# A decoder layer on one core: input projection in three parts, twenty up pairs half ahead, and modulation columns placed by running estimates

## The chip, the cores and the metric

One core of a Trainium2 chip runs the whole layer in one launch. The metric is device time in microseconds, the median of several runs. A profile of one execution stands beside it. TensorE does the matmuls (PE in the rows, PEld for its weight loads), VectorE is DVE, ScalarE is ACT, and SyncE (SP) issues all DMAs of this kernel in one queue.

## What is computed

One layer on 256 tokens of width 2048, all in float32. A conditioning vector c gives six modulation vectors; the layer has eight stick-breaking heads, eight sparse heads with an indexer, an output projection and a gated FFN of width 5504 with a causal convolution of width 3.

```python
mod = silu(c) @ w_ada + b_ada                    # (2048) x (2048, 6 * 2048)
sh1, sc1, g1, sh2, sc2, g2 = split(mod, 6)
h = rmsnorm(x, norm1_g) * (1 + sc1) + sh1
proj = h @ w_in                                  # q, k, v of 8 heads; q, k, v of the sparse heads; indexer
o_sb = stick_breaking_attention(q_sb, k_sb, v_sb)
o_ds = dsa_attention(rope(q_ds), rope(k_ds), v_ds, rope(q_ix), rope(k_ix), w_ix)   # top 64 keys
x = x + g1 * (concat(rmsnorm(o_sb), rmsnorm(o_ds)) @ w_out)
h2 = rmsnorm(x, norm2_g) * (1 + sc2) + sh2
x = x + g2 * ((silu(gate) * val) @ w_down)       # gate, val = split(conv3(h2 @ w_up))
return rmsnorm(x, final_norm_g)
```

## The kernel before

**Numbers in two halves.** Every large matmul is made in fp32r from a high and a low half of each operand. split() (L143) takes a weight tile that load() (L135) has brought into one of four raw buffers: ScalarE casts the high half (L149), VectorE subtracts it for the low half (L150). nat() (L153) and trn() (L175) then issue three matmuls (high by high, high by low, low by high). fold() (L161) does the same with two: one of 512 columns for both halves of the activations and one of 256.

**The modulation vectors.** They are 96 columns of 128 numbers; column j needs 1 MiB of w_ada. ada(j) (L227) loads it and makes the column on VectorE by one multiply with a running sum (L229). ada_pe (L198) makes four columns on TensorE in four steps of 1 MiB; PEG (L44) names those groups, five of them. Columns 0 to 31 are needed by the input projection (k and 16 + k for k-tile k), 32 to 47 by the residual after the output projection, 48 to 79 by the FFN's input (48 + k and 64 + k), and 80 to 95 after the FFN.

**Who places them.** The columns stand in two lists, `pending` and `pend_pe`. pump() (L382) is called between loads; its n-th call emits as many of each list as the n-th digit of two strings in PLAN (L48) says. need(j) (L395) emits until column j is out.

**The input projection** runs in two parts of eight k-tiles (PARTS, L46). do_A (L412) walks the k-tiles of a part and makes h for each (h_make, L339), with eight PSUM banks; do_A2, do_V and do_QK follow with the same k-tiles. put() (L350) copies the sums of the first part to SBUF on ScalarE and adds those of the second part on VectorE.

**Attention.** After A2 of the last part the sparse attention is traced (L522 to L664), then V and QK of the last part with the stick-breaking heads (sb_head, L670). PSUM is split into four banks for sums and four for attention.

**Output projection and FFN.** do_O (L714) runs in two half steps, with the first half of four output tiles ahead of the norm of the stick-breaking heads. resid() (L738) adds the residual and gathers squares; rms_b (L109) and h2_make (L772) then make h2. do_U (L804) makes one pair of up tiles in two halves of eight k-tiles. The first halves of pairs 0 to 7 (G0 = 8, L801) are made first, each holding one PSUM bank, so that only k-tiles 0 to 7 of h2 are needed; then the second halves follow. Pairs 0 to 7 use trn, the others fold. The down projection streams 43 tiles.

**Order.** The program is traced in the order of the code, and a scheduler then puts each engine's instructions in a fixed queue: among those that its own model holds ready it takes the one traced first. On the chip every queue runs in that order.

Of the kernel before, what the change touches and what calls it, by code (L numbers as in the profile page):

```python
# [19 lines left out]
P = 128  # L20
D = 2048
S = 256
# [32 lines left out]
def layer(ctx: ExitStack, tc: tile.TileContext, a, out):  # L55
# [12 lines left out]
    def sm(n, name):  # L68
        return wp.tile([P, n], F32, name=name, tag="sm", bufs=8)

# [37 lines left out]

    def rms_b(sqs_, width, y, name, tag):  # L109
# [25 lines left out]
    def load(src, n, name):  # L135
# [25 lines left out]
    def fold(steps):  # L161

        lo_first = narrow[0] and not any(s[4] for s in steps)
# [32 lines left out]
    def ada_pe(j0, q, st={}):  # L198
# [4 lines left out]
        w = load(a["wg"][PEG.index(j0), q], 2048, f"wg{j0}{q}")  # L203
# [23 lines left out]
    def ada(j):  # L227
        w = load(a["wa"][j], 2048, f"wa{j}")
# [69 lines left out]

    def rope(x, t, H, rd, o, name):
# [12 lines left out]
    def modulate(dh, dl, x, am, rb, sh, name, variant):  # L312

        h = s2([P, S], F32, name)
        if not variant:
# [33 lines left out]

    def put(half, dst, src, scale=1.0):  # L350
# [5 lines left out]
        elif scale == 1.0:  # L356
# [5 lines left out]
    credit = [0.0, 0.0]  # L362
# [17 lines left out]
    step = [0]  # L380

    def pump():  # L382
        i = step[0]
        step[0] += 1
        for c, l in enumerate((pending, pend_pe)):
            if i < len(PLAN[c]):
                n = int(PLAN[c][i])
            else:
                credit[c] += RATE[c]
                n = int(credit[c])  # L390
                credit[c] -= n
            for _ in range(min(n, len(l))):
                emit(l)
# [73 lines left out]
    def do_QK(pi, h):  # L467
        n = PARTS[pi]
        acc = ps(f"QK{pi}{h}", tag=ptag[0])
        if n <= 8:  # L470
            w = load(a[f"wQK_{pi}"][h], 2 * n * P, f"wQK{pi}{h}")
        for p_ in range(2):
            o = p_ * n * P
            if n > 8:
                w = load(a[f"wQK_{pi}"][h][:, o:o + n * P], n * P, f"wQK{pi}{h}{p_}")
                o = 0
            for j0 in range(0, n, 8):
                nj = min(8, n - j0)
                wh, wl = split(w, o + j0 * P, nj * P, f"wQK{pi}{h}{p_}{j0}")
                for j in range(j0, j0 + nj):  # L480
                    trn(acc[:, p_ * S:(p_ + 1) * S], hp(hh, pi, j), hp(hl, pi, j),
                        wh[:, (j - j0) * P:(j - j0 + 1) * P], wl[:, (j - j0) * P:(j - j0 + 1) * P], j == 0, j == n - 1)
# [35 lines left out]
    psum_pool[0] = (pool2, {"acc": 4, "att": 4})  # L518
    ptag[0] = "acc"


    for t in range(NT):  # L522
# [19 lines left out]
    sc_n = [0]  # L542
    pump()

# [5 lines left out]
    for t in range(NT):  # L550
# [27 lines left out]
        V.tensor_tensor(out=sacc[0], in0=sacc[0], in1=sacc[1], op=ALU.add)  # L578
        cur, nxt = sacc
# [7 lines left out]
        V.tensor_tensor(out=mb[t], in0=mb[t], in1=cmt, op=ALU.add)  # L587
        pump()

# [17 lines left out]
    for t in range(NT):  # L607
# [29 lines left out]
        for g in range(2):  # L637
# [6 lines left out]
            for j in range(4):  # L644
                h = 4 * g + j
                A.activation(od[:, h, t * P:(t + 1) * P], pv[:, j, :], AF.Copy, scale=par[:, PDG + h:PDG + h + 1])
        pump()
    for w_ in (4, 2):
# [5 lines left out]

    def norm_o(o, rb_, oh, ol):
# [316 lines left out]
```

## Time and profile before

| what | value |
|---|---|
| median of three runs | 1203.6 us (1203.34 to 1205.74) |
| the profiled execution | 1204.37 us, its span 1202.6 us |
| mean granted TensorE clock | 0.982 |
| TensorE busy | 1150.5 us (96%) |
| VectorE busy | 880.1 us (73%) |
| ScalarE busy | 635.3 us (53%) |
| HBM | 300.24 MB read, 251 GB/s over the span |

A matmul's end is modelled, so a busy TensorE is not TensorE at its peak; the rate is read from the starts. Busy times of VectorE and ScalarE overlap a little from one instruction to the next, so that a duration and the distance of two starts differ. "Idle before" names what ended an engine's wait.

### The profile page before, as it was taken

To read this page: it belongs to the slowest core of one execution; us is meant where nothing else is said; L and a number is where in the kernel's file an instruction comes from. 1 tells how busy PE (TensorE), PEld (TensorE's weight loads), DVE (VectorE), ACT (ScalarE), POOL (GpSimd) and SP (SyncE) were. 2 spreads that over 40 slices of the span, in tenths; PEclk is the share of its full clock that TensorE was granted. 3 is DMA by queue.
4 is the path that set the end of the run, shared out by engine and by line. 5 is a ranking of instruction groups with operands and counts; after the bars stand their busy time and mean duration, and the time that the engine had idled before them with its cause. 6 is when DMAs were issued, how large, how long until landed. Compare 5 with 4: busy or idle time off the path is not lost.

```text
span 1202.6 us, 17743 instructions
## 1 busy us (share of the span) xinstructions
PE 1150.5 (96%) x7120; PEld 1014.9 (84%) x7120; DVE 880.1 (73%) x1267; ACT 635.3 (53%) x1004; POOL 0.2 (0%) x4
## 2 busy tenths in 40 slices
PE   4699999899999998999999999999999999999996
PEld 2578997668879997999888888888888888888885
DVE  4886788699868888978788878787787645545453
ACT  3356554458566444556665565565556544444441
POOL 0000000000000000000000000000000000000000
PEclk9799999999999998999999999999999999999998
DMA  8988989758788796966578657565665555455531
GB/s 321 365 322 318 340 331 350 288 198 328 279 314 321 295 344 250 353 227 231 187 283 313 229 207 264 211 241 213 242 214 184 201 180 202 179 193 193 181 135 70
DMA packets 43283, 303.49 MB, mean 252 GB/s; under 512 B 4928, under 2 KB 5440, under 8 KB 7232
## 3 DMA queue, kind: packets, MB, share of 16 engines
q1 hardware_dynamic: 43200, 302.35, 68.2%
q8 instruction: 56, 0.92, 0.3%
q14 instruction: 27, 0.22, 0.0%
HBM read 300.24 MB, written 2.10 MB: 251 GB/s over the span
## 4 chain that ended last, share of the span: by engine, by line
PE 91%; DVE 4%; ACT 3%; DMA 1%; issue 1%; SPq 0%; DVEq 0%
PE U L172 21%; PE W L172 13%; PE U L170 11%; PE W L170 7%; PE U L178 3%; PE U L179 3%; PE QK L177 3%; PE U L177 3%; PE O L177 3%; PE O L179 3%; PE O L178 3%; PE QK L178 3%; PE QK L179 3%; PE A L155 2%; DVE wa L229 2%; PE A L156 2%
## 5 line engine op out<-in xcount | busy, mean ns | idle before, releaser
L229 DVE SCALAR_TENSOR_TENSOR wa<-wa,scb 128x2048 f32<-128x2048 f32 x76 | 173.4, 2284 | 2.2 <-DMA wa<-wa 2.1
L848 ACT COPY u<-U 128x256 f32<-128x256 f32 x70 | 26.1, 372 | 116.6 <-PE U L172 116.6
L849 DVE TENSOR_TENSOR u<-U,u 128x256 f32<-128x256 f32 x70 | 29.4, 420 | 58.7 <-ACT u L848 58.7
L859 DVE SCALAR_TENSOR_TENSOR uc<-u,par,uc 128x255 f32<-128x255 f32 (+1 forms) x140 | 63.8, 478 | 0.9
L855 ACT ACTIVATE uc<-u,par 128x256 f32<-128x256 f32 x70 | 41.9, 601 | 0.0
L866 ACT CAST aT<-uc 128x256 fp32r<-128x256 f32 x43 | 17.4, 404 | 33.3 <-DVE uc L865 33.3
L894 DVE SCALAR_TENSOR_TENSOR x1T<-W,mod,x1T 128x256 f32<-128x256 f32 x16 | 7.7, 482 | 31.1 <-PE W L170 31.1
L745 ACT ACTIVATE x2q<-x1T 128x256 f32<-128x256 f32 x15 | 6.3, 418 | 38.7 <-DVE x1T L740 38.6
L327 ACT ACTIVATE amul<-mod,b,par 128x1 f32<-128x1 f32 x32 | 12.0, 385 | 27.7 <-DVE wa L229 27.7
L206 PE MATMUL ap<-wg,csil 128*32 128x512 f32 x160 | 24.0, 657 | 0.7 <-DMA wg<-wg 0.4
L861 ACT ACTIVATE uc<-uc 128x256 f32<-128x256 f32 x43 | 17.9, 416 | 7.7 <-DVE uc L859 7.6
L330 ACT ACTIVATE mod<-mod,par 128x1 f32<-128x1 f32 x32 | 8.7, 295 | 24.0 <-DVE wa L229 22.9
L865 DVE TENSOR_TENSOR uc<-uc 128x256 f32<-128x256 f32 x43 | 18.2, 423 | 2.8
L867 DVE TENSOR_TENSOR aT<-uc,aT 128x256 fp32r<-128x256 f32 x43 | 18.0, 418 | 0.8 <-ACT aT L866 0.7
L859 DVE SCALAR_TENSOR_TENSOR uc<-U,par,uc 128x255 f32<-128x255 f32 (+1 forms) x32 | 15.0, 478 | 1.0 <-ACT uc L855 0.6
L206 PEld LDWEIGHTS ap<-wg,csil 128*32 128x32 f32 x160 | 4.4, 116 | 9.8 <-issue 7.4
L559 PE MATMUL rel<-ws,qixT 64*128 64x128 f32 (+1 forms) x64 | 9.7, 399 | 1.5 <-ACT rl L564 1.5
L576 DVE SCALAR_TENSOR_TENSOR scw<-rl,wix,scw 128x128 f32<-128x128 f32 (+1 forms) x28 | 10.4, 409 | 0.0
L287 PE MATMUL cb<-ident,csil 128*128 128x128 f32 x16 | 3.6, 423 | 7.1 <-DMA ident<-ident 7.1
L211 ACT COPY rw<-ap 128x512 f32<-128x512 f32 x5 | 2.9, 586 | 14.1 <-PE ap L206 14.1
L155 PE MATMUL A<-wA00h,hh 128*128 128x512 f32 x4 | 2.5, 671 | 8.1 <-ACT hh L322 8.1
L855 ACT ACTIVATE uc<-U,par 128x256 f32<-128x256 f32 x16 | 9.0, 560 | 2.3 <-DVE uc L859 2.3
(2810 smaller groups left out, 4025.3 us busy)
## 6 DMA issues: line engine op xcount, KB each, us to landing
wU<-wU SPq DMA_DIRECT2D x86, 1024.0 KB, 4.8
wa<-wa SPq DMA_DIRECT2D x76, 1024.0 KB, 5.8
wD<-wD SPq DMA_DIRECT2D x43, 1024.0 KB, 4.6
wg<-wg SPq DMA_DIRECT2D x20, 1024.0 KB, 7.2
wA<-wA SPq DMA_DIRECT2D x16, 1024.0 KB, 7.4
wQK<-wQK SPq DMA_DIRECT2D x16, 1024.0 KB, 6.6
wO<-wO SPq DMA_DIRECT2D x16, 1024.0 KB, 6.9
xT<-xT SPq DMA_DIRECT2D x4, 512.0 KB, 5.8
```

Source lines behind the costliest of these rows:

```text
L155: T.matmul(pt, lhsT=xh, rhs=wh, start=first, stop=False)
L170: T.matmul(pt[:, 1, :], lhsT=wl, rhs=x[:, 0, :], start=False, stop=stop)
L172: T.matmul(pt, lhsT=wh, rhs=x, start=first, stop=stop)
L177: T.matmul(pt, lhsT=wh, rhs=xh, start=first, stop=False)
L178: T.matmul(pt, lhsT=wh, rhs=xl, start=False, stop=False)
L179: T.matmul(pt, lhsT=wl, rhs=xh, start=False, stop=last)
L206: T.matmul(pt[32 * j:32 * j + 32, :], lhsT=csil[:, k:k + 1].to_broadcast([P, 32]), rhs=w[:, j * 512:(j + 1) * 512], start=q == 0, stop=q == 3)
L229: i = V.scalar_tensor_tensor(out=w, in0=w, scalar=1.0, in1=scb, op0=ALU.mult, op1=ALU.mult, accum_out=mod[:, j:j + 1])
L848: A.copy(out=u[:, gv, :], in_=acc[gv][:, 1, :])
L849: V.tensor_tensor(out=u[:, gv, :], in0=acc[gv][:, 0, :], in1=u[:, gv, :], op=ALU.add)
L855: A.activation(uc[:, gv, :], u[:, gv, :], AF.Identity, scale=par[:, PCW + 3 * i + 2:PCW + 3 * i + 3], bias=par[:, PCB + i:PCB + i + 1])
L859: V.scalar_tensor_tensor(out=uc[:, gv, sft:S], in0=u[:, gv, 0:S - sft], scalar=par[:, o:o + 1], in1=uc[:, gv, sft:S], op0=ALU.mult, op1=AL ...
```

## The change

The input projection runs in three parts of 4, 6 and 6 k-tiles. The first halves of 20 up pairs, not 8, are made ahead; each is copied from PSUM to a tile `ut` in SBUF at once, and the second half is added to it. PEG keeps two groups, 40 and 44, and they may be emitted only once the input projection's A stages are over (`open_pe`). PLAN is gone: pump() now keeps three running estimates, of TensorE's, VectorE's and the DMA's time (`clk`), which every traced step advances (`spend`), and emits a column when the DMA and VectorE are estimated far enough ahead of TensorE. V of the last part is traced ahead of the sparse attention. The sparse attention, the heads, put, resid, rope, the norms and the modulation of h2 are marked: traced within tc.high_priority(), so that the scheduler takes them ahead of unmarked instructions that are ready. PSUM is split five to three in the middle stage, and five output tiles have their first half ahead.

```diff
-PEG = [4, 40, 48, 76, 52]
-PARTS = [8, 8]
-PLAN = ("40300000010011011020201102100000000000000010222000110020002020001010003012011002101000000000100000213",
-        "00000000000000000000000000000110010000001200000100001200003100000000000000110100001010001000001000000")
-RATE = (0.4, 0.7)
+PEG = [40, 44]
+PARTS = [4, 6, 6]
+G0 = 20
...
+    def ahead(f):
+        def g(*args, **kw):
+            with tc.high_priority():
+                return f(*args, **kw)
+        return g
...
+    clk = {"pe": 0.0, "dve": 0.0, "dma": 8.0}
+    def spend(pe=0.0, dve=0.0):
+        clk["pe"] += pe
+        clk["dve"] = max(clk["dve"], clk["pe"] - 10.0) + dve
+    def load(src, n, name, weight=True):
+        if weight:
+            pump()
+        clk["dma"] = max(clk["dma"], clk["pe"] - 14.0) + 3.04 * n / 2048
+        if weight:
+            clk["pe"] = max(clk["pe"], clk["dma"] + 5.0)
+            spend(0.0, 2.45 * n / 2048)
         w = wp.tile([P, 2048], F32, name=name, tag="raw", bufs=4)
...
     def nat(pt, xh, xl, wh, wl, first, last):
+        spend(3 * (pt.shape[-1] + 32) / 2400)
...
     def trn(pt, xh, xl, wh, wl, first, last):
+        spend(0.36)
...
     def ada(j):
-        w = load(a["wa"][j], 2048, f"wa{j}")
+        w = load(a["wa"][j], 2048, f"wa{j}", False)
+        spend(0.0, 2.4)
...
     def pump():
-        i = step[0]
-        step[0] += 1
-        for c, l in enumerate((pending, pend_pe)):
-            if i < len(PLAN[c]):
-                n = int(PLAN[c][i])
...
+        for _ in range(2):
+            if clk["dma"] + 11.5 > clk["pe"]:
+                return
+            if pending and clk["dve"] + 6.0 <= clk["pe"]:
+                emit(pending)
             else:
+                if pend_pe and open_pe[0]:
+                    emit(pend_pe)
+                return
...
-        natural(pi, a[f"wV_{pi}"][g], 512, 4, acc, f"V{pi}{g}")
+        natural(pi, a[f"wV_{pi}"][g], 512, 4 if PARTS[pi] % 4 == 0 else 3, acc, f"V{pi}{g}")
...
-    psum_pool[0] = (pool2, {"acc": 4, "att": 4})
+    psum_pool[0] = (pool2, {"acc": 5, "att": 3})
     ptag[0] = "acc"
+    open_pe[0] = True
+    for g in range(2):
+        do_V(last_p, g)
+    begin()
     for t in range(NT):
         rope(a2[:, t, 0:ID].rearrange("p (h d) -> p h d", h=1)[:, :, 0:16], t, 1, 16, 32, f"ki{t}")
...
-    for g in range(2):
-        do_V(last_p, g)
     for h in range(NH):
         do_QK(last_p, h)
...
-    acc = [ps(f"O{m}", tag="acc") for m in range(4)]
-    for m in range(4):
+    acc = [ps(f"O{m}", tag="acc") for m in range(5)]
+    for m in range(5):
...
-    G0 = 8
-    uacc = {}
+    uacc, ut = {}, []
     def do_U(f, i):
-        if i == 0:
-            uacc[f] = [bank(f"U{f}{gv}") for gv in range(2)] if f >= G0 else bank(f"U{f}")
+        if f < G0:
+            uacc[f] = bank(f"U{f}{i}")
+        elif i == 0:
+            uacc[f] = [bank(f"U{f}{gv}") for gv in range(2)]
...
     for f in range(G0):
         do_U(f, 0)
-        pump()
+        if f % 4 == 0:
+            ut.append(b8([P, 4, 2, S], F32, f"ut{f}"))
+        A.copy(out=ut[-1][:, f % 4, :, :], in_=uacc.pop(f))
...
         else:
-            u = acc
+            u = ut[f // 4][:, f % 4, :, :]
+            V.tensor_tensor(out=u, in0=acc, in1=u, op=ALU.add)
```

begin() and end() open and close the same mark around the sparse attention; pump() is called between an end() and the next begin(). put, rms_b, rope, norm_o, sb_head, resid and the modulate of h2 are wrapped by ahead().

## Rows read from the trace of the kernel before

**Rows 1.** The page's first part: busy us, share of the span, instructions.

```profile
span 1202.6 us, 17743 instructions
...
PE 1150.5 (96%) x7120; PEld 1014.9 (84%) x7120; DVE 880.1 (73%) x1267; ACT 635.3 (53%) x1004; POOL 0.2 (0%) x4
```

**Rows 2.** Busy time by stage: length, engines' busy us, PEclk, DMA share, GB/s.

```profile
0.00:57.00 57.00, 29.54 (x111) 19.66 (x112) 36.40 (x78) 22.28 (x40) 0.20 (x4) 0.85 0.90 342
57.00:92.80 35.80, 33.94 (x145) 26.44 (x144) 27.84 (x34) 20.39 (x34) 0.00 (x0) 1.00 0.88 333
92.80:168.00 75.20, 75.20 (x529) 71.44 (x528) 57.95 (x57) 43.77 (x71) 0.00 (x0) 1.00 0.86 324
168.00:222.00 54.00, 53.75 (x262) 43.69 (x264) 40.64 (x46) 22.61 (x33) 0.00 (x0) 1.00 0.91 339
222.00:262.00 40.00, 34.73 (x208) 22.35 (x201) 34.70 (x129) 19.50 (x35) 0.00 (x0) 0.91 0.61 232
...
372.00:458.00 86.00, 86.00 (x720) 86.00 (x719) 74.55 (x89) 42.80 (x63) 0.00 (x0) 1.00 0.87 322
...
466.00:511.70 45.70, 45.37 (x363) 45.08 (x363) 44.35 (x59) 22.79 (x36) 0.00 (x0) 0.95 0.83 314
511.70:557.80 46.10, 46.10 (x386) 46.10 (x386) 36.82 (x57) 27.86 (x43) 0.00 (x0) 1.00 0.64 233
```

**Rows 3.** TensorE in order of time, 5 to 60 us: start, us, instruction.

```profile
34.27 1.22 PE L155 MATMUL A<-wA00h,hh 128*128 128x512 f32 x2 [8.10 <-ACT hh L322]
...
56.88 0.39 PE L155 MATMUL A<-wA20h,hh 128*128 128x512 f32 x1
...
57.56 0.39 PE L155 MATMUL A<-wA20h,hh 128*128 128x512 f32 x1
```

**Rows 4.** Other engines in order of time, first 30 us.

```profile
4.49 2.60 SPq L137 DMA_DIRECT2D wg<-wg  x4
...
12.99 1.55 ACT L288 COPY scb<-cb 128x512 f32<-128x512 f32 x3
...
14.69 0.68 DVE L197 TENSOR_TENSOR sq<-sq 128x512 f32<-128x512 f32 x1
...
29.71 2.29 DVE L229 SCALAR_TENSOR_TENSOR wa<-wa,scb 128x2048 f32<-128x2048 f32 x1 [0.79 <-DMA wa<-wa]
```

**Rows 5.** The chain that ended last, one up pair of 35: start, us.

```profile
564.19 3.83 PE U L170 x32
568.02 7.28 PE U L172 x32
```

**Rows 6.** TensorE in order of time, 220 to 263 us.

```profile
221.76 1.92 PE L206 MATMUL ap<-wg,csil 128*32 128x512 f32 x16
224.39 0.66 PE L214 MATMUL aq<-ident,rw 128*128 128x128 f32 x4 [0.71 <-ACT rw L211]
...
235.40 0.79 PE L155 MATMUL V<-V1000h,hh 128*128 128x512 f32 x1
```

**Rows 7.** VectorE in order of time: split, two columns, partial sums, convolution steps.

```profile
55.43 1.23 DVE L150 TENSOR_TENSOR wA21l<-wA,wA21h 128x1024 fp32r<-128x1024 f32 x1 [0.39 <-ACT wA21h L149]
56.57 2.28 DVE L229 SCALAR_TENSOR_TENSOR wa<-wa,scb 128x2048 f32<-128x2048 f32 x1
...
58.78 2.29 DVE L229 SCALAR_TENSOR_TENSOR wa<-wa,scb 128x2048 f32<-128x2048 f32 x1
...
207.93 2.48 DVE L357 TENSOR_TENSOR qix<-A,qix 128x512 f32<-128x512 f32 x4
...
554.14 0.99 DVE L859 SCALAR_TENSOR_TENSOR uc<-U,par,uc 128x255 f32<-128x255 f32 x2
...
556.92 0.42 DVE L867 TENSOR_TENSOR aT<-uc,aT 128x256 fp32r<-128x256 f32 x1
```

**Rows 8.** DMA issues: count, KB each, median us to landing.

```profile
wQK<-wQK SPq DMA_DIRECT2D x16, 1024.0 KB, 6.6
...
xT<-xT SPq DMA_DIRECT2D x4, 512.0 KB, 5.8
```

More of the change, by code (lines that the diff above doesn't have):

```diff
@@ L69, in sm, with begin, end @@
         return wp.tile([P, n], F32, name=name, tag="sm", bufs=8)
+    def ahead(f):
[3 more added lines that the diff above has]
+        return g
+    guard = []
+    def begin():
+        guard.append(tc.high_priority())
+        guard[-1].__enter__()
+    def end():
+        guard.pop().__exit__(None, None, None)
     psum_pool = [None]
@@ L107, in rb @@
         return wp.tile([P, S], F32, name=name, tag="rb", bufs=2)
+    @ahead
     def rms_b(sqs_, width, y, name, tag):
@@ L161, in fold @@
     def fold(steps):
+        spend(0.348 * len(steps))
         lo_first = narrow[0] and not any(s[4] for s in steps)
@@ L202, in ada_pe @@
         pt = st[j0]
-        w = load(a["wg"][PEG.index(j0), q], 2048, f"wg{j0}{q}")
+        w = load(a["wg"][PEG.index(j0), q], 2048, f"wg{j0}{q}", False)
+        spend(0.85 if q < 3 else 1.4)
         for j in range(4):
@@ L297, in layer @@
                            op1=ALU.mult)
+    @ahead
     def rope(x, t, H, rd, o, name):
@@ L314, in modulate @@
         h = s2([P, S], F32, name)
+        spend(0.0, 0.9)
         if not variant:
@@ L348, in layer @@
     qk = [b8([P, 8, S], F32, f"qk{i}") for i in range(2)]
+    @ahead
     def put(half, dst, src, scale=1.0):
@@ L355, in put @@
                 A.mul(out=dst, in_=src, mul=scale)
-        elif scale == 1.0:
+            return
+        spend(0.0, 0.53)
+        if scale == 1.0:
             V.tensor_tensor(out=dst, in0=src, in1=dst, op=ALU.add)
@@ L378, in emit @@
             emitted.update(range(j, j + 4))
-    step = [0]
+    open_pe = [False]
     def pump():
-        i = step[0]
-        step[0] += 1
-        for c, l in enumerate((pending, pend_pe)):
-            if i < len(PLAN[c]):
-                n = int(PLAN[c][i])
-            else:
[L389 to L393, printed above, removed]
+        for _ in range(2):
[3 more added lines that the diff above has]
+                emit(pending)
+            else:
+                if pend_pe and open_pe[0]:
+                    emit(pend_pe)
+                return
     def need(j):
@@ L469, in do_QK @@
         acc = ps(f"QK{pi}{h}", tag=ptag[0])
-        if n <= 8:
-            w = load(a[f"wQK_{pi}"][h], 2 * n * P, f"wQK{pi}{h}")
+        w = load(a[f"wQK_{pi}"][h], 2 * n * P, f"wQK{pi}{h}")
         for p_ in range(2):
-            o = p_ * n * P
-            if n > 8:
-                w = load(a[f"wQK_{pi}"][h][:, o:o + n * P], n * P, f"wQK{pi}{h}{p_}")
+            if p_ == 0 or n > 4:
+                wh, wl = split(w, p_ * n * P, min(2, 8 // n) * n * P, f"wQK{pi}{h}{p_}")
                 o = 0
[L477 to L482, printed above, removed]
+            else:
+                o = n * P
+            for j in range(n):
+                sl = slice(o + j * P, o + (j + 1) * P)
+                trn(acc[:, p_ * S:(p_ + 1) * S], hp(hh, pi, j), hp(hl, pi, j), wh[:, sl], wl[:, sl], j == 0, j == n - 1)
         dst = qk[h // 4]
@@ L542, in layer @@
     sc_n = [0]
+    end()
     pump()
+    begin()
     def sc_t(L, name):
@@ L587, in layer @@
         V.tensor_tensor(out=mb[t], in0=mb[t], in1=cmt, op=ALU.add)
+        end()
         pump()
+        begin()
     for t in range(NT):
@@ L646, in layer @@
                 A.activation(od[:, h, t * P:(t + 1) * P], pv[:, j, :], AF.Copy, scale=par[:, PDG + h:PDG + h + 1])
+        spend(10.0, 5.0)
+        end()
         pump()
+        begin()
     for w_ in (4, 2):
@@ L653, in layer @@
     odl = b8([P, NH, S], F32R, "odl")
+    @ahead
     def norm_o(o, rb_, oh, ol):
@@ L661, in norm_o @@
             V.tensor_tensor(out=ol[:, sl, :], in0=o[:, sl, :], in1=oh[:, sl, :].bitcast(F32), op=ALU.subtract)
+            spend(0.0, 2.5)
     norm_o(od, rdb, odh, odl)
+    end()
     pump()
+    begin()
+    end()
     os_ = b8([P, NH, S], F32, "os")
     sbt = b8([P, D], F32, "sbt")
+    @ahead
     def sb_head(h):
+        spend(3.0, 1.6)
         q = qk[h // 4][:, (h % 4) * 2, :]
@@ L736, in layer @@
     sq2 = ws[:, 1536:1792]
+    @ahead
     def resid(dst, acc, gate, res, sqsum, k, name):
+        spend(0.0, 0.9)
         resid_i[0] = V.scalar_tensor_tensor(out=dst, in0=acc, scalar=gate, in1=res, op0=ALU.mult, op1=ALU.add)
@@ L780, in h2_make @@
         sh = mod_cols(k, 64, 48, am, PN2, b2)
-        modulate(h2[k // 4][:, k % 4, 0, :], h2[k // 4][:, k % 4, 1, :], x1T[i][:, j, :], am, r2p if k < 3 else r2, sh,
+        ahead(modulate)(h2[k // 4][:, k % 4, 0, :], h2[k // 4][:, k % 4, 1, :], x1T[i][:, j, :], am, r2p if k < 3 else r2, sh,
                  f"g2_{k}", False)
@@ L821, in do_U @@
                 else:
-                    trn(uacc[f][:, gv, :], x[:, 0, :], x[:, 1, :], wh[:, sl], wl[:, sl], k == 0 and gv == 0,
-                        k == KT - 1 and gv == 1)
+                    trn(uacc[f][:, gv, :], x[:, 0, :], x[:, 1, :], wh[:, sl], wl[:, sl], j == 0 and gv == 0,
+                        j == 7 and gv == 1)
         fold(steps)
```

7 lines of the change are left out of this document (3 added, 4 removed).

## The prediction

> **What bounds the kernel now.** I read the page's first part, then busy time by stage, then the stretches in which TensorE is not gapless. TensorE is busy for 1150.5 of the span's 1202.6 us, VectorE for 880.1 [rows 1]. By stage [rows 2], TensorE has almost no idle time from 57 us on: 1.9 us up to 92.8, 0.3 in 168 to 222, none in the output projection (372 to 458) and none in the second up halves (511.7 to 557.8). From there to the last down matmul it streams one up pair in 7.28 + 3.83 = 11.11 us [rows 5]. So the time moves in three ways only: less TensorE work, less idle time ahead of 57 us, or less loss in the attention stretch (222 to 262). Three resources stand just behind it: the DMA engines move 324 to 342 GB/s (0.86 to 0.91 of their time) in each stage up to 222, and VectorE is busy 74.6 of 86.0 us in the output projection and 44.4 of 45.7 us in the first up halves [rows 2]. A change that hands them work can lose what TensorE gains.
>
> At the start TensorE begins the A projection at 34.27 us and only at 56.88 has it done two k-tiles [rows 3]. A k-tile is 24 matmuls of 512 columns; three take 57.56 - 56.88 = 0.68 us at the full clock, so it is 5.44 us of work, and 22.6 us went by for 10.9.
>
> **The change, part by part.** The sum is made against the profiled execution, 1204.4 us (span 1202.6 and 1.8 around it), 0.8 above the median of 1203.6.
>
> *Start.* PEG loses group 4, so four 1 MiB loads that are issued at 4.49 us leave the head of SP's queue [rows 4] and the first two modulation columns take their place. VectorE can begin them when ScalarE's last scb copy ends (12.99 + 1.55 = 14.5) and its own square sums end (14.69 + 0.68 = 15.4). Two columns at 2.21 us start to start [rows 7] end at 19.8; today the first matmul comes 34.27 - 32.00 = 2.3 us after the second column [rows 3, 4], so A starts at about 22.5 instead of 34.3. Each further k-tile needs 3 MiB (two columns, one wA): 3.15 MB at 342 GB/s [rows 2] is 9.2 us; VectorE needs 2 x 2.21 + 2 x 1.14 and two modulation steps of 0.4, some 7.5 us, so the DMA sets the pace. Part 0 now ends after four k-tiles: 22.5 + 3 x 9.2 + 5.4 = 55. At 55 four are done where two were at 56.9: **12.8 us ahead** (2 x 5.44 + 1.9). Bounds 9 and 15: A starting 3 us later, or 373 GB/s (below).
>
> *Parts of 6 and 6.* While TensorE does A2, V and QK of part 0 (37.6 us: 3.7, 10.9 and 23.0, by their columns and the matmul rates of [rows 2, 3]), the DMA must bring their weights and the columns of part 1. From k-tile 3 on to the weights of k-tile 9 that is 1.3 + 2 + 4 + 12 + 6 = 25.3 MiB, or 26.5 MB; at 324 GB/s, the lowest rate of these stages, 82 us, at 339 / 0.91 = 373, all engines busy all the time, 71 us [rows 2], where TensorE has 37.6 + 32.6 = 70 us of work. For part 2 it is 29 MiB in 82 to 94 us against 89. Stall 1 to 17; at 342 it is 7.5 and 0, I take **8 us lost**. Stepping the new planner's three clocks through the loads gives the order: 6 of part 1's 12 columns are issued ahead of its A stage, 8 of part 2's 12; the rest come within it. Extra partial sums on VectorE, 30 of them, are 14 us by the row of four in 2.48 us for the wide ones [rows 7] and an estimated 0.35 for QK's at half that width; VectorE was busy 40.6 of 54.0 us in 168 to 222 [rows 2], so they fit, and cost 0 to 4 us, in the far bound.
>
> *PE groups.* Outside the start four groups become two. A group is 32 matmuls, twice 1.92, and its transposes, 0.66 [rows 6], with 0.7 us of wait between: 4.5 to 5.2 us. **9.3 us gained.** In return twelve more columns go to VectorE and SP carries the same bytes; 12 x 2.21 = 26.5 us, whose cover is the far larger time until the second up halves: G0 = 20 gives 20 first halves, 115 us, to the last sixteen columns. Today there are eight, 46 us.
>
> *Attention.* In 222 to 262 TensorE idles 5.3 us and its granted clock is 0.91, so some 7 us at the lower level (1.2 GHz) [rows 2], and the first V matmul comes only at 235.40 [rows 6]. Now V of the last part is traced ahead of the attention, so 16 us of matmuls stand there without waiting. The loss of about 8.7 us can come back between 0 and 6; **3 gained**. The marks move instructions within their queues and add none; what a marked instruction waits for, everything behind it on ScalarE or VectorE waits for too, split() above all, and TensorE behind that.
>
> *Up pairs.* Twelve more pairs use trn, three matmuls of 256 columns, in place of fold. trn takes 86.00 / 720 = 0.119 us per matmul [rows 2], 0.358 per step; fold 11.11 / 32 = 0.347 [rows 5]. 12 x 32 x 0.011 to 0.013 = **4.6 us lost** (4.2 to 5). The Trainium skill (TensorE: Matmul & The Clock Gate, Back-to-back issue gap) gives 262 cycles for 256 columns and 518 for 512, by which both forms need 0.325 to 0.328 us a step and the switch would cost 1 us, the sum 3.6 us less. The trace has both forms slower than that and the three-matmul one more so; I stay with the trace.
>
> *VectorE behind the first 20 pairs.* A second half below G0 now has a 512-wide addition. Start to start: two splits 2.28, four convolution steps 1.82 to 1.98, two short ones 0.68 to 0.84, the addition 0.62 to 0.69 [rows 7]: 5.4 us of the 5.73 us of its 48 matmuls, 5.9 if nothing overlapped. ScalarE's ut copy of 0.6 us is hidden by its low load (27.9 of 46.1 us [rows 2]). In the output projection the planner's clocks place 14 columns; 11 ran there today, so VectorE goes from 74.6 to about 81 of 86. Cost 0 to 16; **2 us lost**, near the low end, since VectorE was busy for 97% of 466 to 511.7 and TensorE idled 0.3 us there [rows 2].
>
> Sum: 12.8 - 8 + 9.3 + 3 - 4.6 - 2 = 10.5 us; 1204.4 - 10.5 = **1194 us**.
>
> **The rivals.**
> *VectorE takes TensorE's place (slower).* For about 200 us (output projection and 20 second halves) it would be 92 to 95% full, and marked resid, put and head chains stand ahead of the splits. If such a chain makes VectorE wait once per weight tile, the 0.3 to 0.4 us of slack is spent, and each further 0.5 us lands on TensorE, 36 tiles in all: 18 us, 1212. It decides from an added wait of 0.4 us a tile. For it: today's waits of an addition or a copy on its partner (the chain through two engines) are already there. Against: the 97% stretch.
>
> *Small loads starve the projection (about as before).* Part 0's QK loads are 0.5 MiB and share four raw buffers with the columns: 14 loads in 23 us leave a buffer 6.6 us, where 1 MiB takes 6.6 us to land and 0.5 MiB took 5.8 [rows 8], and the split 2.3 more. Then some 7 us of loading are lost, and with the stall halfway to its far end (4 more) the time is 1205; with one of the two, 1198 to 1201. The Trainium skill (DMA: Bandwidth & Descriptors, Rules for kernel authors) asks for at least 1 MiB per DMA, which speaks against parts of 4 and 6; no row here shows a stream of 0.5 MiB loads.
>
> *Everything is covered (more than forecast).* Stall 4, attention 6, VectorE nothing: 1194 - 4 - 3 - 2 = 1185. *The marks do nothing*: the attention term is 0, 1197, inside the forecast's own range.
>
> **How the numbers follow.** Forecast (1188 to 1201) 0.52; covered, below 1188, 0.13; small loads, 1201 to 1206, 0.12; VectorE, above 1206, 0.23. A measurement of this kernel can tell 0.2%, 2.4 us, from no change: faster 0.65 (the first two), same 0.12 (the third), slower 0.23. The range that leaves out 2 in 10 is 1184 to 1213.
>
> **What would show it.** Start: the first A matmul near 22 us and the first A2 matmul near 55 instead of 92.8. Parts: gaps of 3 to 5 us ahead of the last two or three k-tiles of part 1, released by ScalarE or VectorE behind a load. Groups: 64 ap matmuls, not 160, and 88 columns on VectorE. Attention: V matmuls between the last A2 and the first rel, and the granted clock at 1.0. Up: first halves starting at about 447 instead of 466, second halves at about 562, and pair 20 at about 677, where pair 20 today starts at 691 (557.8 + 12 x 11.11). If VectorE binds, gaps of 0.3 us or more stand in front of trn matmuls in the second halves, released by the splits, and pair 20 comes after 691. I am wrong at the root if A starts after 30 us, or if the DMA moves under 320 GB/s up to 220 us.

## The result, and the profile after

The changed kernel takes 1222.0 us (median of four, 1219.9 to 1226.3) against 1204.5 us for the kernel before, a ratio of 1.0143, 95% interval 1.0126 to 1.016: slower by some 17 us, where 1194 was forecast. The profiled execution has a span of 1224.5 us. Executions of one kernel differ by up to 8 us, and the one profiled here is the slowest of its four, so medians decide between kernels and the traces show where the time lies.

The page's first part answers to [rows 1], and the groups of the fifth part say what became of the columns (88 on VectorE) and of the groups (64 matmuls):

```profile
span 1224.5 us, 18424 instructions
...
PE 1154.0 (94%) x7396; PEld 1038.7 (85%) x7396; DVE 923.7 (75%) x1326; ACT 634.9 (52%) x1009; POOL 0.2 (0%) x4
...
L261 DVE SCALAR_TENSOR_TENSOR wa<-wa,scb 128x2048 f32<-128x2048 f32 x88 | 201.1, 2287 | 22.6 <-DMA wa<-wa 22.3
...
L237 PE MATMUL ap<-wg,csil 128*32 128x512 f32 x64 | 11.0, 600 | 0.0
```

To see where the time went, cut both executions at three events: the end of the last A2 matmul, the last operation that norms the stick-breaking heads (osl), and the first up matmul. Columns as in [rows 2]. The kernel before:

```profile
0.00:221.80 221.80, 192.23 (x1042) 161.12 (x1045) 162.63 (x211) 109.06 (x175) 0.20 (x4) 0.96 0.89 334
221.80:385.70 163.90, 158.32 (x1064) 127.03 (x1064) 134.48 (x262) 102.52 (x218) 0.00 (x0) 0.98 0.78 291
385.70:465.60 79.90, 75.02 (x623) 74.53 (x621) 66.62 (x83) 38.33 (x58) 0.00 (x0) 0.99 0.83 300
465.60:949.50 483.90, 483.54 (x3009) 438.77 (x3010) 390.12 (x570) 279.82 (x432) 0.00 (x0) 0.99 0.66 239
```

The changed kernel:

```profile
0.00:242.50 242.50, 205.62 (x1106) 177.19 (x1106) 194.45 (x262) 116.30 (x188) 0.20 (x4) 0.97 0.85 311
242.50:410.40 167.90, 151.80 (x973) 123.74 (x974) 136.80 (x266) 95.22 (x212) 0.00 (x0) 0.94 0.69 255
410.40:482.30 71.90, 66.28 (x537) 65.36 (x536) 54.34 (x72) 33.04 (x51) 0.00 (x0) 0.95 0.70 252
482.30:971.60 489.30, 488.90 (x3393) 459.18 (x3394) 411.71 (x584) 284.71 (x437) 0.00 (x0) 0.99 0.71 255
```

The up projection starts at 482.3 where about 447 was forecast: 35 us are lost ahead of it. It then lasts 5.4 us longer than before. The prediction gives no time for the last A2, but its terms do. From the first A2 matmul (58.1) to the last:

```profile
58.10:242.50 184.40, 173.48 (x985) 152.10 (x984) 150.91 (x177) 88.46 (x141) 0.00 (x0) 0.97 0.84 306
```

TensorE is busy for 173.5 us, some 5 of them lost to a granted clock of 0.97, so there are 168 us of work. The prediction's 55 for the first A2, this work and its stall of 8 make 231. So 3 us are lost at the start and 8 more as stall (10.9 idle and some 5 of clock, in place of 8). The other 24 are lost behind the last A2, where 216 us were forecast and 239.8 went by; before it was 243.8.

How far one profile can be trusted shows in e3 below. Its TensorE, VectorE and ScalarE run the same instructions in the same order up to the up projection, and there the last A2 ends at 237.6 and the up projection starts at 473.7. By the same sums, 10 us of stall and 20 us behind the last A2 are left of the 16 and 24.

*Behind the last A2* TensorE does have less to do: 218.1 us busy in the two middle rows, 233.3 before. But it idles 21.7 us (167.9 - 151.8 + 71.9 - 66.3) where it idled 10.5, and its granted clock fell from 0.98 and 0.99 to 0.94 and 0.95. It was at the lower level (1.2 of 2.4 GHz, a granted clock of 0.50) for 25.6 us, busy in 16.9 of them, against 8.8 and 6.8 before; half of the busy time is what that costs, 8.4 us against 3.4. So the work at the full clock fell by 20.2 us (15.2 + 5.0), 11.2 came back as idle time and 5.0 as clock, and 4.0 were left. In the long stretch no engine is full: TensorE is busy 90% of it, VectorE 81%. Its first 40 us came out as hoped and the rest did not. The change's two parts, then the kernel before in the second:

```profile
242.50:282.50 40.00, 37.15 (x208) 24.61 (x208) 36.37 (x116) 17.43 (x33) 0.00 (x0) 1.00 0.62 216
282.50:410.40 127.90, 114.64 (x766) 99.13 (x766) 100.43 (x152) 77.79 (x179) 0.00 (x0) 0.93 0.72 267
...
262.00:385.70 123.70, 123.39 (x857) 104.57 (x857) 99.58 (x133) 83.03 (x184) 0.00 (x0) 1.00 0.83 309
```

In the second part TensorE is busy 8.8 us less, and it takes 4.2 us more.

*Up to the last A2* the DMA moved 311 GB/s where the kernel before moved 334. It is 75.4 MB in 242.5 us; at 334 GB/s the same bytes would take 225.8.

What ended TensorE's waits, the changed kernel, up to the last A2 and then up to the first up matmul (us in total, times, longest):

```profile
PE A L183 <- ACT hh L356: 12.9, 6, 3.3
PE cb L319 <- DMA ident<-ident: 7.8, 1, 7.8
PE r1b L143 <- DVE r1y L140: 5.3, 1, 5.3
...
PE rsbb L143 <- DVE rsby L140: 2.8, 1, 2.8
PE O L207 <- ACT osh L707: 2.8, 1, 2.8
PE U L207 <- ACT h L351: 2.8, 1, 2.8
PE QK L209 <- DVE wQK200l L177: 2.6, 1, 2.6
PE QK L207 <- ACT wQK260h L176: 2.4, 1, 2.4
```

Six first matmuls of a k-tile wait for a normed tile (hh), that is for a column, mod, amul and two steps more. Behind the last A2 the gaps are in the heads (QK) and at their norm (rsbb, O).

In the up projection nothing waits, so the main rival has no place there: TensorE is busy all of the first halves and all of the second, with VectorE at 105 of 115.4 us:

```profile
482.30:597.60 115.30, 115.29 (x940) 115.00 (x941) 93.86 (x101) 61.01 (x89) 0.00 (x0) 0.98 0.87 326
597.60:713.00 115.40, 115.40 (x964) 115.40 (x963) 105.08 (x173) 74.34 (x117) 0.00 (x0) 1.00 0.54 193
```

### The profile page after: what moved, and what is told of

Read it like the earlier page. It is cut to its first block, busy times and chain, and to the rows that moved or that the text cites. A ratio compares the mean times of both kernels' runs of the same rounds, so it can differ in the third digit from the quotient of the medians.

```text
span 1224.5 us, 18424 instructions
## 1 busy us (share of the span) xinstructions
PE 1154.0 (94%) x7396; PEld 1038.7 (85%) x7396; DVE 923.7 (75%) x1326; ACT 634.9 (52%) x1009; POOL 0.2 (0%) x4
## 4 chain that ended last, share of the span: by engine, by line
PE 59%; DVE 2%; DMA 1%; ACT 0%; issue 0%; DVEq 0%; SPq 0%
PE W L201 13%; PE U L201 13%; PE W L199 7%; PE U L199 7%; PE U L207 6%; PE U L208 6%; PE U L209 6%; DMA wa<-wa 1%; DVE wa L261 0%; DVE x1T L957 0%; DVE uc L916 0%; PE O L208 0%; PE O L209 0%; PE O L207 0%; PE r2p L129 0%; PE r3p L129 0%
## 5 line engine op out<-in xcount | busy, mean ns | idle before, releaser
L261 DVE SCALAR_TENSOR_TENSOR wa<-wa,scb 128x2048 f32<-128x2048 f32 x88 | 201.1, 2287 | 22.6 <-DMA wa<-wa 22.3
L916 DVE SCALAR_TENSOR_TENSOR uc<-u,par,uc 128x255 f32<-128x255 f32 x92 | 42.0, 477 | 0.3
L905 DVE TENSOR_TENSOR u<-U,u 128x256 f32<-128x256 f32 x46 | 19.4, 422 | 28.8 <-ACT u L904 28.8
L912 ACT ACTIVATE uc<-u,par 128x256 f32<-128x256 f32 x46 | 27.7, 601 | 13.7 <-DVE u L905 13.7
L916 DVE SCALAR_TENSOR_TENSOR uc<-ut,par,uc 128x255 f32<-128x255 f32 (+1 forms) x80 | 33.2, 478 | 0.0
L912 ACT ACTIVATE uc<-ut,par 128x256 f32<-128x256 f32 x40 | 21.8, 593 | 0.1
L908 DVE TENSOR_TENSOR ut<-U,ut 128x512 f32<-128x512 f32 x20 | 13.8, 691 | 6.4 <-PE U L209 6.4
L890 ACT COPY ut<-U 128x512 f32<-128x512 f32 x20 | 11.6, 580 | 0.1
L237 PE MATMUL ap<-wg,csil 128*32 128x512 f32 x64 | 11.0, 600 | 0.0
L355 ACT ACTIVATE h<-h,mod,amul 128x256 f32<-128x256 f32 x16 | 9.6, 600 | 0.8 <-DVE h L354 0.4
```

Of the source, the lines that this page charges most:

```text
L261: i = V.scalar_tensor_tensor(out=w, in0=w, scalar=1.0, in1=scb, op0=ALU.mult, op1=ALU.mult, accum_out=mod[:, j:j + 1])
L905: V.tensor_tensor(out=u[:, gv, :], in0=acc[gv][:, 0, :], in1=u[:, gv, :], op=ALU.add)
L912: A.activation(uc[:, gv, :], u[:, gv, :], AF.Identity, scale=par[:, PCW + 3 * i + 2:PCW + 3 * i + 3], bias=par[:, PCB + i:PCB + i + 1])
L916: V.scalar_tensor_tensor(out=uc[:, gv, sft:S], in0=u[:, gv, 0:S - sft], scalar=par[:, o:o + 1], in1=uc[:, gv, sft:S], op0=ALU.mult, op1=AL ...
```

## The experiments

Times are medians with the ratio to the kernel before in the same session; the changed kernel stands at 1222.0, 1.0143 (1.0126 to 1.016). Diffs are against the changed kernel unless the text says otherwise.

**Parts undone one at a time.**

*e1: two parts.*

```
-PARTS = [4, 6, 6]
+PARTS = [8, 8]
```

> The changed kernel with the input projection back in two parts of eight k-tiles; all else stays. Theory A (the three parts lose the time: smaller loads through four raw buffers, 17 us less of the last part left to fill the attention): 1202 to 1208, the last A2 ends with the projection's lost time down from about 22 us to under 14, and TensorE does not stand idle for 5 us at the norm of the stick-breaking heads. Theory B (the marks lose it): 1216 to 1224, the norm's idle time stays. Theory C (the planner's column placement loses it, whatever the parts): 1214 to 1222.

1218.2 us, 1.0105 (1.0087 to 1.0124). That is far above what it would be if the three parts were the main cause: they cost some 4 us, net of all that goes with them. The DMA moves 322 GB/s up to the last A2, and TensorE still waits 15.9 us for hh. Loads of 1 MiB alone don't bring 334 back.

*e2: no marks.* `ahead`, `begin` and `end` do nothing.

```
-            with tc.high_priority():
-                return f(*args, **kw)
+            return f(*args, **kw)
```

> The changed kernel with every mark taken off (nothing is traced at high priority); all else stays. Theory A (three parts): 1219 to 1225, no change beyond noise. Theory B (marked instructions hold up the splits behind them): 1205 to 1212, with VectorE's and TensorE's waits in the attention stretch down by 10 us. Theory C (column placement): 1219 to 1225.

1223.8 us, 1.0152 (1.0135 to 1.017): not distinguishable from the changed kernel. Gaps move (7.4 us ahead of the sparse attention's keys, less in the heads) and the time stays.

*e3: eight pairs in halves, as before.*

```
-G0 = 20
+G0 = 8
```

> The changed kernel with eight up pairs half ahead instead of twenty; all else stays. If the twelve pairs cost only their extra matmul time (my sum: 4.6 us, the trace of the changed kernel: about 5), this gains 5 us where the sixteen last columns fit in 46 us, but they need 16 x 2.2 = 35 us of VectorE beside 23 us of splits, 12 us too much: 1224 to 1232. If the columns were not late, 1215 to 1218.

1241.8 us, 1.0303 (1.0283 to 1.0323). TensorE waits once, at the first second half:

```profile
PE U L207 <- ACT wU010h L176: 26.2, 1, 26.2
```

Ahead of that split, ScalarE's small steps wait 28 us for columns on VectorE. With columns as late as the new planner sends them, more than eight pairs are needed (14 are enough in e16).

*e4: V of the last part behind the sparse attention.* The loop of two `do_V` goes back to just ahead of the heads.

> The changed kernel with V of the last part traced behind the sparse attention again, as before the change; all else stays. My sum gave the new place 3 us (0 to 6): then this is 1222 to 1228. If V ahead of the attention only holds up the marked chain, and its loss of 6 us idle at 242 to 290 us comes from there: 1214 to 1219.

1224.4 us, 1.016 (1.0138 to 1.0183): 2.3 us slower by the medians, the intervals overlap.

**Columns: who does them, and when.**

*e5 and e7: PE groups back.*

```
-PEG = [40, 44]
+PEG = [4, 40, 48, 76, 52]     e5
+PEG = [4, 40, 44]             e7
```

> The changed kernel with the five modulation groups on TensorE of the kernel before (4, 40, 48, 76, 52) in place of two (40, 44); parts, marks and the order of the pairs stay as changed. Theory columns (the loss ahead of the up projection is the modulation work that moved to VectorE and came late there, group 4 at the start above all): time falls by 8 to 15 us, to 1207 to 1214, and the columns behind by 5 fewer at 142 us. Rival emission (the pacing by estimates sends columns too late whatever engine does them): within 4 us of the changed kernel, 1218 to 1225. Rival cover (the loss is work used up under the attention): the groups 48, 52 and 76 add 8 matmuls of weight groups each and TensorE is the bound, so 1222 to 1232.

> The changed kernel with one modulation group more on TensorE, group 4 (columns 4 to 7, the shifts of the second four k-tiles) at the start; 40 and 44 stay. Theory columns at the start: the group costs some 6 us of matmuls but its four columns are not waited for, A of the second part starts 3 to 6 us earlier, the time falls by 3 to 7 us, to 1215 to 1219. Theory emission: the same number of forced columns elsewhere, 1220 to 1224. Rival cost (the group's TensorE time is paid in full where its cover is gone): 1226 to 1230.

1234.8 us, 1.0244 (1.0222 to 1.0266), and 1237.7 us, 1.0273 (1.0244 to 1.0303). Both came out above even their dearest rival. Group 4 is forced just ahead of the second part, where TensorE waits 3.3 us for its loads in e5; behind the last A2, in e5 the stretch is 162.5 us, but the groups that come late put 85.0 us between the normed heads and the up projection (71.9 in the change). What lengthened e7 was not followed. The groups are no remedy under this planner.

*e6: all columns earlier.*

```
-            if clk["dma"] + 11.5 > clk["pe"]:
+            if clk["dma"] + 5.5 > clk["pe"]:
-            if pending and clk["dve"] + 6.0 <= clk["pe"]:
+            if pending and clk["dve"] + 1.0 <= clk["pe"]:
```

> The changed kernel with the pacing of the modulation columns loosened: a column may go when the modelled DMA is 5.5 us ahead of TensorE (11.5 in the change) and VectorE's model 1 us (6 in the change). Theory emission (columns are sent late, and each forced one exposes a column, mod, amul, hh chain of about 3 us to TensorE): the idle time of TensorE on hh falls from 22 us by half or more, and the time by 5 to 12 us, to 1210 to 1217. Theory columns as work: no change, 1219 to 1225. Rival DMA (weights are late because the rate is 304 to 326 GB/s, and columns sent earlier take their place): slower, 1225 to 1235.

1335.7 us, 1.1073 (1.1043 to 1.1104): 114 us slower. The DMA moves 347 and 353 GB/s, more than the 334 of the kernel before, and TensorE idles over a quarter of the time:

```profile
100.00:200.00 100.00, 74.41 (x340) 59.19 (x338) 87.25 (x99) 38.44 (x71) 0.00 (x0) 0.90 0.94 347
200.00:300.00 100.00, 69.63 (x364) 60.12 (x365) 82.63 (x93) 26.56 (x48) 0.00 (x0) 0.85 0.94 353
```

Columns that nobody needs yet go by the same queue and the same four buffers as the weights. The rival was right in kind, off in size by ten.

*e9: the first columns behind the first norm.*

```
-    rms_b([sq1[0][:, 0, :], sq1[0][:, 1, :]], D, r1, "r1", "ps")
+    after[0], _ = rms_b([sq1[0][:, 0, :], sq1[0][:, 1, :]], D, r1, "r1", "ps")
```

> The changed kernel with one edge added: no modulation column starts on VectorE before the last small operation of the first norm. In the changed kernel two columns (2.3 us each) stand ahead of it and TensorE waits 5.3 us there. Theory start (what is lost in the first 30 us is lost for good): A starts at 22 to 24 us in place of 27.0 and the time falls by 3 to 5 us, to 1217 to 1219. Rival chain (the columns come 3 to 5 us later, so A waits for them in place of the norm, or behind its first k-tiles): A starts at 25 to 28, the time stays, 1220 to 1224. Rival queue (all later columns slide too): slower by 2 to 4, 1224 to 1227.

1222.5 us, 1.0146 (1.0122 to 1.017). The wait for the norm goes and its place is taken in full by the wait for the columns:

```profile
19.76 0.69 PE L143 MATMUL r1b<-ident,r1y 128*128 128x128 f32 x2 [1.17 <-DVE r1y L140]
26.46 1.22 PE L183 MATMUL A<-wA00h,hh 128*128 128x512 f32 x2 [6.01 <-ACT hh L356]
```

A starts at 26.5 instead of 27.0: two columns, the norm, a split and the modulation share VectorE.

**Cover for the gaps behind the last A2.**

*e8: two O first halves held for the norm of the heads.*

```
+        if hold[0]:                  in trn, first matmul i
+            order(i, nrm[0])         nrm[0]: last matmul of the norm's sums
-    for m in range(5):
+    for m in range(3):               m = 3, 4 after rms_b("rsb"), with hold[0] set
```

> The changed kernel with the first halves of two output tiles (m = 3 and 4, 96 matmuls, some 12 us) held on TensorE until the sums of the stick-breaking norm have been issued, so that they lie beside the norm's chain. In the changed kernel TensorE idles 5.6 us there (2.8 for the norm's small operations, 2.8 for the first half of the normed heads) and runs at half clock behind it. Theory cover (the gap is there because its filler was used up earlier under the heads, which did not need it): the gap goes to under 1 us, the time falls by 5 to 8 us, to 1214 to 1217. Rival moved gap (the heads, with the two halves less to fill, idle as much as the norm did): idle up to the up projection unchanged, 1220 to 1224. Rival held too long (weights of the two halves sit in their buffers and block the loads behind them): 1225 to 1230.

1226.8 us, 1.0179 (1.0156 to 1.0202). The gaps at rsbb and O are gone and stand in the heads instead (sums, then outputs):

```profile
PE u L743 <- DVE sbt L741: 5.0, 2, 2.6
...
PE o L749 <- ACT sbt L747: 2.4, 2, 1.2
```

The stretch lasts 169.7 us (167.9), its granted clock is 0.90 (0.94). The mechanism is that of "moved gap": filler moved from one place of the stretch is missing at another. The time lies above its 1224, in the range of "held too long", which the gaps don't show.

*e10: the two groups not before the heads.* `open_pe[0] = True` moves to just ahead of the loop over heads.

> The changed kernel with its two modulation groups on TensorE (40 and 44) allowed only from the stick-breaking heads on; in the changed kernel they go at 248 to 307 us, under the sparse attention, and the heads have none, where the kernel before issues three groups at 306 to 370 us. Theory filler (what was saved on groups was not saved, since in the heads they lay in gaps): the gaps of 2.6, 2.4 and 5.6 us in the heads and behind them shrink by half or more, the time falls by 3 to 7 us, to 1215 to 1219. Rival (the sparse attention then has the gaps): unchanged, 1220 to 1224. Rival late columns (40 to 47 are the gates of the attention's residual, needed from the first output tile on): 1225 to 1230.

1228.5 us, 1.0196 (1.0175 to 1.0218); the stretch lasts 174.1 us. "Filler" fell: in the heads TensorE now waits 8.2 us in three gaps for the sums (u). The time is that of "late columns", but no run checks its mechanism.

**Parts of the change alone, in the kernel before.**

*b1: only the 20 pairs.* Against the kernel before: G0 = 20 with the tiles `ut`, the copy and the addition of the change; plan, parts, groups and marks as before.

> The kernel before with one part of the change alone: 20 up pairs in halves in place of 8, the first halves copied to SBUF and added to the second; its planner, parts, groups and marks stay. Theory of the prediction's term (36 us of narrow matmuls in three wide passes in place of two, nothing given back, since the kernel before waits for no column there): slower by 4.5 to 6, 1209.5 to 1211. Rival equal passes (the Trainium skill, TensorE: Matmul & The Clock Gate, Back-to-back issue gap): slower by 1 to 2, 1206 to 1207. Rival gain (fewer folds, fewer small copies on ScalarE, columns due later): 1200 to 1204.

1221.9 us, 1.0142 (1.0119 to 1.0165): 15.5 us slower, where the term said 4.6. The up projection takes 500.1 us, 16.2 more. VectorE is full where the second halves begin, and TensorE waits 6 us for its splits in these two rows, at a clock of 0.73 in the first:

```profile
606.00:617.00 11.00, 6.88 (x38) 6.47 (x37) 10.33 (x17) 4.75 (x8) 0.00 (x0) 0.73 0.68 226
617.00:675.00 58.00, 55.99 (x461) 55.56 (x460) 56.05 (x91) 38.13 (x59) 0.00 (x0) 0.99 0.69 250
```

TensorE idles 6.4 us in this up projection and is busy for 493.5 us, 9.9 more than before, in which the term's 4.6 and the lower clock behind the waits lie. So "VectorE takes TensorE's place" is a real mechanism of these pairs. It shows with the old plan, which runs five columns (11.4 us) on VectorE between 606 and 675 us, and not in the changed kernel, which runs two beside its second halves.

*b2: only the marks, V ahead and the banks.* Against the kernel before.

> The kernel before with the marks on the short chains, the last part's V ahead of the sparse attention and the five and three banks, but with its own hand-set plan, parts, groups and pairs. Theory (these are worth in the change what taking them away cost there, 1.7 and 2.3 us): faster by 1.5 to 4, 1201 to 1203.5. Rival no idle to win (the kernel before idles only 5.9 us between 230 and 463): within 1 us, 1204 to 1206. Rival displaced plan (the plan counts steps, and V's steps now come before the attention's, so its columns and groups come at other places): slower by 2 to 6, 1207 to 1211.

1214.6 us, 1.0083 (1.0061 to 1.0105): slower by 8, all of it ahead of the up projection, which starts at 478.0. That is more than "displaced plan" said. The hand-set plan counts steps, and V's steps now come first, so this run does not price the marks by themselves.

**Is the stretch behind the last A2 a chain?** In every trace up to here it lasted 162 to 176 us, whatever lay in it.

*e11: parts of 4, 4 and 8.* TensorE's work is the same; V and QK of two k-tiles move from ahead of the last A2 to behind it.

```
-PARTS = [4, 6, 6]
+PARTS = [4, 4, 8]
```

> The changed kernel with parts of 4, 4 and 8 k-tiles in place of 4, 6 and 6. TensorE's work is the same; V and QK of two k-tiles (some 17 us) move from ahead of the last A2 to behind it, beside the attention. Theory chain (from the last A2 to the normed heads takes 162 to 170 us whatever lies beside it): the last A2 ends 12 to 17 us earlier, at 225 to 230 (242.5 in the change), the normed heads come at 392 to 398 (410.4), the up projection starts at 466 to 474 (482.3), time 1206 to 1214. Rival sum (TensorE's work and its idle time are what counts, wherever it lies): the up projection starts within 3 us of 482, time 1219 to 1225. Rival loads (QK of two 4-k-tile parts is loaded in pieces of half a MiB, twice as many): 1225 to 1232.

1216.8 us, 1.0099 (1.0082 to 1.0116), 5.3 us faster than the change, with intervals apart:

```profile
0.00:231.10 231.10, 189.66 (x986) 160.61 (x986) 187.25 (x251) 109.71 (x176) 0.20 (x4) 0.93 0.86 314
231.10:394.70 163.60, 154.44 (x1032) 128.10 (x1033) 139.37 (x264) 97.88 (x210) 0.00 (x0) 0.99 0.73 273
394.70:472.50 77.80, 72.66 (x600) 71.74 (x598) 65.66 (x83) 37.10 (x57) 0.00 (x0) 0.97 0.81 299
```

The last A2 ends 11.4 us earlier (6.5 against e3's profile). The two rows behind it hold 122 matmuls more, the 17 us of V and QK that moved, and together they last 241.4 us against 239.8 (236.1 in e3). "Sum" falls by the medians; it had no gain. The gain stays under the forecast; TensorE waits 17.6 us for hh here, 12.9 in the change.

*e12 and b3: half of the selection rounds,* in the changed kernel and in the kernel before.

```
-        for r in range(8):
+        for r in range(4):
```

> The changed kernel with 4 of the 8 rounds that select the largest scores left out for both token tiles (16 operations on VectorE, 5.5 us in all; the mask then keeps half as many). No matmul, load or column goes. Theory chain: the whole chain behind it comes 5 us earlier, time 4 to 6 us less, 1216 to 1218. Rival sum (TensorE's work and the column work bound the stretch): under 2 us, 1220 to 1224.

> The kernel before with the same 4 of 8 selection rounds left out (5.5 us of VectorE). There TensorE idles only 5.9 us from the last A2 to the up projection, so its work covers the chain. Theory chain: no or little gain, 0 to 1.5 us, 1203 to 1206. Rival (VectorE's work itself is the bound in that stretch in both): 4 to 6 us less, 1199 to 1202.

1217.8 us, 1.0109 (1.0089 to 1.0128): 4.3 us off the changed kernel by the medians, the intervals just touching, for 5.5 us of VectorE work, with no matmul less. 1208.3 us, 1.0014 (1.0002 to 1.0026): nothing off the kernel before. Its stretch, and that of the shortened change:

```profile
223.80:390.90 167.10, 161.96 (x1063) 127.96 (x1064) 129.53 (x238) 102.41 (x218) 0.00 (x0) 0.98 0.76 284
...
240.90:402.40 161.50, 149.24 (x973) 119.33 (x974) 128.18 (x241) 94.69 (x211) 0.00 (x0) 1.00 0.71 259
```

(The first line is the kernel before with half of the rounds, the second the change.) Before, TensorE is busy 97% of it and covers the chain; in the change a shorter chain is a shorter time. VectorE has less work in both runs, so these two alone don't tell a chain from VectorE's load.

*e6 and e3 read again* settle that. In e6 the columns go so early that none lies in this stretch. Its row, and that of e3, which has the change's own queues:

```profile
345.50:510.20 164.70, 148.02 (x973) 121.91 (x974) 102.40 (x232) 93.33 (x203) 0.00 (x0) 0.93 0.41 149
...
237.60:401.60 164.00, 147.93 (x974) 120.11 (x974) 136.76 (x266) 95.25 (x212) 0.00 (x0) 0.97 0.72 261
```

With a quarter of VectorE's work gone, at 149 GB/s, and with no weight among the things that TensorE waits for, the stretch lasts as long. So neither VectorE's load nor the weights set its length. TensorE's work doesn't either: it is busy for 148.0 us here, and was for 158.3 in the 163.9 us of the kernel before. TensorE's longest waits are then inside the heads and behind them (u 5.0, O 2.8, o 2.7 us).

**Can the columns be in time?** All with parts 4, 4, 8.

*e14, e15, e16: earlier columns for the input projection alone; then fewer pairs.*

```
+            d, v = (8.0, 3.0) if pending and pending[0][0] < 32 else (11.5, 6.0)
-            if clk["dma"] + 11.5 > clk["pe"]:
+            if clk["dma"] + d > clk["pe"]:
-            if pending and clk["dve"] + 6.0 <= clk["pe"]:
+            if pending and clk["dve"] + v <= clk["pe"]:
```

e15 has (5.5, 1.0) there; e16 is e14 with `G0 = 14`.

> Parts 4, 4, 8, and the pacing loosened for the columns of the input projection alone (columns 0 to 31; modelled margins 8 us for DMA and 3 us for VectorE in place of 11.5 and 6). Theory late columns: the DMA between 97 and 160 us goes from 300 GB/s to 320 or more, the idle time on the normed tiles from 17.6 us to under 12, the last A2 ends at 222 to 227 (231.1 without it), time 1207 to 1213. Rival DMA (weights are displaced one for one): 1214 to 1220.

> As the run with margins 8 and 3, with 5.5 and 1.0 for columns 0 to 31: the margins of the run that lost 113 us when they stood for all columns. Theory late columns: as good or better, 1205 to 1213. Rival DMA (a column taken by a modelled margin of 5.5 us displaces a weight that is wanted at once; the 32 columns are all done by 160 us, and the projections before that starve): 1220 to 1240, with idle time on loaded weights, not on normed tiles.

> As the run with margins 8 and 3, with 14 up pairs in halves in place of 20. Each pair in halves costs 5.5/12 = 0.46 us more on TensorE, so 6 fewer give back 2.8 us; 26.2 us of waiting with 8 pairs, less 6 x 5.8 of first halves, is nothing with 14. Theory: 2 to 3.5 us faster than that run. Rival (the columns of the second k-tiles of the second norm come as late as the second halves want them): no gain or up to 8 us slower.

1225.7 us, 1.0169 (1.0145 to 1.0193); 1255.1 us, 1.0414 (1.0385 to 1.0442); 1222.0 us, 1.0133 (1.0114 to 1.0152). In e14 the wait for hh fell from 17.6 to 7.2 us as expected, but the DMA moved 311 GB/s between 97 and 160 us, not 320, and the last A2 ended at 232.2, no earlier. The waits stand on weights now (up to the last A2):

```profile
PE A L183 <- ACT hh L356: 7.2, 3, 3.1
...
PE B L184 <- DVE B100l L177: 4.1, 1, 4.1
PE V L183 <- ACT V0000h L176: 2.3, 1, 2.3
```

The time is above even the DMA rival's. The stretch behind takes 176.2 us, with 21 columns and 1093 matmuls in it, where e11 has 17, 1032 and 163.6 us. e15, with its last A2 at 259.9, shows the same more strongly. e16's up projection takes 486.8 us, e14's 489.1: 2.3 us for six pairs, 0.38 a pair, and no wait with 14.

No version tried beats the kernel before.

## Why the prediction was wrong

**The step that failed: counting TensorE's work behind the last A2 as time.** The sum let some 28 us fall away there (243.8 to 216): V and QK of two k-tiles done earlier, fewer groups, 3 us in the attention. The work did go, 20 us of it, and 4 us of time with it. For the attention, the heads and their norm are dependent work over TensorE, ScalarE and VectorE; the stretch went from 163.9 to 167.9 us. Before, work beside it kept TensorE 97% busy, so it read as TensorE's time: the row gave the busy share and did not show what comes up when that share is taken out. e11 and e12 show it from two sides: 17 us of matmuls put back cost 2 to 5 us there, VectorE operations taken out win there, and b3 shows that they win nothing in the kernel before. e6 shows that the length stays where no engine is near full but TensorE at 90%. Which steps make it up is open: it never fell below 161 us. With 20 or 21 columns in it, where the change has 16, it was 176 to 181 (e1, e14, e15, e16), but those four also have 1093 matmuls in it where the change has 973, so which of the two lengthens it is not shown.

**Parts, -8.** Mechanism right, the size near its far end of 17: 16 us of stall in the profile, 10 in e3's. I took 324 to 342 GB/s from [rows 2]; it was 317 up to 220 us, under the 320 that I had named as wrong at the root. The rate was the old plan's as much as the DMA's: SP's loads wait for the four buffers, mostly for columns to be done on VectorE. From 30 to 220 us, before and after:

```profile
SPq L137 <- DVE wa L229: 66.0, 22, 7.4
...
SPq L164 <- DVE wa L261: 55.4, 22, 5.6
```

Those waits did not grow. What else lowered the rate is argued, not shown: the loads came in smaller pieces (a 0.75 MiB QK load fills a buffer as a 1 MiB load does), and columns were sent when they were already wanted. The rule of the Trainium skill (DMA: Bandwidth & Descriptors, Rules for kernel authors), at least 1 MiB per DMA, points the right way at most: e1, with 1 MiB QK loads, moves 322 GB/s up to its last A2, and e3, e8 and e12, with the change's loads, 313 to 319. e1 is 4 of the 17 us faster, by all that two parts bring; the size of a load has no price of its own here.

**Start, +12.8: 9.7.** A began at 27.0, not 22.5, and A2 at 58.1, not 55. The first column started on VectorE at 18.5, not 15.4, behind the first small operation of the norm, and the norm's others queue behind the two columns; e9 shows that either order gives 26.5 to 27.

**PE groups, +9.3: not gained.** The time is off TensorE (11.0 us for the two that are left), but of the 128 matmuls of the four groups outside the start all but 20 lay behind the last A2, beside the chain. e10 and e5 show that placing or restoring groups under this planner only costs.

**Attention, +3: gained in its place and lost again.** In the first 40 us behind the last A2 TensorE idles 2.9 us at the full clock, where it idled 5.3 at 0.91 and, with V behind the attention again (e4), 7.9 at 0.83. The second part of the stretch gives it back, so that by the whole time V ahead is worth 2.3 (e4) and the marks at most 1.7 (e2), neither clear of its interval.

**Up pairs, -4.6: right in the change.** 5.4 by the two up projections, 4.6 by e16's 0.38 x 12. My estimate from the figures that the Trainium skill (TensorE: Matmul & The Clock Gate, Back-to-back issue gap) gives for an isolated matmul was 1; the traces bear out the row.

**VectorE behind the pairs, -2: nothing.** 115.4 us of second halves without a gap. The time came out in that rival's range, but it was lost in another place; b1 has the rival's mechanism.

**Small loads** came nearest of the rivals: the projection did starve, though no run shows that the size of the loads did it. Its 1198 to 1205 leaves out all that was lost behind the last A2. My range took each term's bounds and no bound for the claim that a stretch at 97% has nothing else under it.

## What to carry to other kernels

A stretch where one engine is 97% busy may still be a dependent chain that this engine's other work covers. Before work is taken out of it, find the chain's own length by shortening the chain, or by taking filler away, in one run each. And work moved ahead of the event that starts such a chain delays the whole chain: move it beside the chain, as e11 did for 5.3 us.

## What the runs showed of the hardware

Short gaps on TensorE can cost more than themselves. In the changed kernel, two gaps of 2.8 us end at 404.8 and 408.0, and a stretch at the lower level lies around the second:

```profile
395.00:405.50 10.50, 7.40 (x54) 6.50 (x52) 7.58 (x12) 5.11 (x11) 0.00 (x0) 1.00 0.71 272
405.50:412.30 6.80, 3.81 (x16) 3.52 (x17) 4.70 (x4) 2.22 (x3) 0.00 (x0) 0.50 0.22 90
412.30:419.00 6.70, 6.70 (x58) 6.70 (x58) 3.61 (x5) 2.72 (x4) 0.00 (x0) 1.00 0.30 99
```

A granted clock of 0.50 is 1.2 GHz of 2.4, for 6.8 us; TensorE is busy in 3.8 of them, so this cost 1.9 us. The stretches from 289.4 and from 337.2 us begin in the same way, within a gap of 2.6 us and 0.5 us behind one of 2.4. Not every such gap is followed by one: in e12 a gap of 2.4 us that ends at 323.6 is not. Over the two rows behind the last A2 the clock cost 5.0 us more than before, beside 11.2 us of added idle time. The forecast had the clock only as something to win back in the attention.
